# A decoder block on one core: one quarter of a projection moved ahead of the first scores, q and k transfers shared by two queues, and two ScalarE copies placed further back

## The chip, the core and the metric

The kernel runs on one core of a Trainium2 chip. Such a core has five engines that run their own instruction streams in order: TensorE (PE, matrix products, with its weight loads listed as PEld), VectorE (DVE), ScalarE (ACT), GpSimd (POOL) and SyncE (SP). SP and POOL mostly issue DMAs here. The metric is the device time of the whole program in microseconds (us); less is better. The time of a kernel is the median of its runs.

## What is computed

One layer of a decoder block on 256 tokens of width 1024, all in float32. Cut to what matters:

```python
h = rms_norm(x, attn_norm_g)
proj = h @ w_in                      # q,k,v of branch a, q,k,v of branch b, f, g
qa, ka = (partial_rope(rms_norm(split_heads(t, 8), gain)) for t in (qa, ka))
o_a = causal softmax attention(qa, ka, va)       # 8 heads of 64; one block of 256
qb, kb = (rms_norm(split_heads(t, 8), gain) for t in (qb, kb))
c = cumsum(log_sigmoid(f + b_forget))
o_b = causal softmax attention(qb, kb, vb), scores + c[t] - c[s]
gates = sigmoid(g + b_gate)
x = x + (gates[0] * (o_a @ w_branch_moba) + gates[1] * (o_b @ w_branch_fox)) @ w_out
u, g = split(rms_norm(x) @ w_ffn_up);  g = causal_depthwise_conv(g, 3 taps)
x = x + (silu(g) * u) @ w_ffn_down
```

With 256 tokens and blocks of 256 the block selection of branch a selects nothing beyond the token's own block, so branch a is plain causal attention.

## The kernel before

**Weights.** All weights come as chunks of 1 MB (128 x 2048), in the order of the list `chunks`: six projections `qkv` 0 to 5 (q, k, v of branch a, then q, k, v of branch b; two chunks each), eight gate chunks `wg` 0 to 7, then the later matrices. `load` issues a chunk's DMA on SP's queue into one of three buffers `raw`, and cuts it into two quarters of 1024 columns (a quarter of a projection each). Each quarter is split on chip into a high part (`whi`, a copy on ACT, line 134) and a low remainder (`wlo`, a subtraction on DVE, line 135), so that three fast products stand in for one float32 product. `use` asks for a quarter and loads five quarters further ahead (`AHEAD`). The six buffers of `whi` and `wlo` come free as PE finishes quarters.

**Order.** PE's order is that of the code. On DVE, ACT, POOL and SP a scheduler orders the instructions when the program is built, by their place in the code and by its own estimate of when they become ready; `after(i, j)` adds that `i` may not be placed ahead of `j`.

**The stage that the change touches.** `project(m, pt, h)` multiplies two quarters of projection `m` into two PSUM banks; a quarter is 12 matrix products of 128x512. There are 8 banks in all. `finish_qk` normalises a projected q or k: squares on ACT, sums and scalings on DVE, which frees the two banks. `start_turn` transposes 32x32 blocks on DVE and then moves the blocks with 16 DMAs of 32 KB from one half of the tile `pp` to the other; `end_turn` copies the result with a gain on ACT into `qT0`, `kT0`, `qT1` or `kT1` (the digit is the branch). The names `q0`, `k0` are branch a, `q1`, `k1` branch b.

PE's order around the change: k of branch b is projection 4. Three of its four quarters are multiplied, then the small product of `forget_c` (cumulative sum, one bank, which DVE then copies at line 361), then the scores of branch a for three pairs of heads (`scores(0, pair)`, two banks a pair, needing `qT0` and `kT0`), then the fourth quarter, then v of branch b (projection 5), `gate(0)`, the transposes of probabilities `turn(0, 0)` and `turn(0, 1)`, the fourth pair's scores, `gate(1)`, `gate(2)`, `gate(3)`, `turn(0, 2)` and `turn(0, 3)`, and then branch b's scores (`first_half`, `second_half`). A `gate` is two quarters of a gate chunk's projection, and two of them share two banks; DVE moves the result out at line 484 (into `lead`).

For branch a the 16 DMAs of a `start_turn` go alternately to POOL's and SP's queue; for branch b all 16 go to POOL's.

Of the kernel before, what the change touches and what calls it, by code (L numbers as in the profile page):

```python
# [11 lines left out]
AF = mybir.ActivationFunctionType  # L12
ALU = mybir.AluOpType
AX = mybir.AxisListType
# [9 lines left out]
NH = 8  # L24
# [18 lines left out]
def decoder_block(ctx, tc, a, out):  # L43
    nc = tc.nc
# [6 lines left out]
    def T(shape, tag, bufs=1, dt=F32):  # L51
        return sb.tile(shape, dt, tag=tag, bufs=bufs, name=tag)
# [34 lines left out]
    state = {"next": 0, "raw": None, "ahead": AHEAD, "hold": False, "behind": None}  # L87

    def after(i, j):
        tc.add_manual_dep(i.ins, j.ins.name, mybir.DependencyInfo(mybir.DependencyClass.NoSync, mybir.DependencyReason.DATA), reason="order")  # L90
# [25 lines left out]
    def load(upto):  # L116
        while state["next"] <= min(upto, 2 * len(chunks) - 1):
            i, h = divmod(state["next"], 2)
            state["next"] += 1
            if i < 2:  # L120
                lead(2 * i + h)
                continue
            c = chunks[i]
            if h == 0:
                w = 1024 if i == 2 else 2048
                src = a[c[0]]
                for j in (c[1] - (c[0] == "qkv"), *c[2:]):
                    src = src[j]
                raw = state["raw"] = T([P, 2048], "raw", RB)
                for j in range(2048 // w):  # L130
                    nc.sync.dma_start(raw[:, j * w:(j + 1) * w], src[:, j * w:(j + 1) * w])
            raw = state["raw"][:, h * 1024:(h + 1) * 1024]
            hi, lo = home(2 * i + h)
            whi = nc.scalar.activation(hi, raw, AF.Copy)  # L134
            wlo = nc.vector.tensor_tensor(lo, raw, hi.bitcast(F32), op=ALU.subtract)  # L135
            if state["behind"]:
                for i, j in zip((whi, wlo), state["behind"]):
                    if j:
                        after(i, j)
            split[c, h] = (hi, lo, whi)  # L140

    def use(c, h):
        if not state["hold"]:
# [8 lines left out]
    def col(c, n=1):  # L152
        return sm[:, c:c + n]
# [36 lines left out]
    mask3 = cst[:, 384:768]  # L190
# [46 lines left out]
    def project(m, pt, h, quarters=(0, 1)):  # L237
        for hh in quarters:
            wh, wl = use(("qkv", m, h) if isinstance(m, int) else m, hh)
            for k2 in range(2):  # L240
                k = 4 * h + 2 * hh + k2
                rh, rl = (pairs(w[:, k2 * 512:(k2 + 1) * 512]) for w in (wh, wl))
                parts = ((xh, rh), (xl, rh), (xh, rl)) if m == 0 else ((xh, rh), (xh, rl), (xl, rh))
                for i, (lhs, rhs) in enumerate(parts):
                    for t in range(NT):
                        nc.tensor.matmul(pt[t], lhs[:, k, t * P:(t + 1) * P], rhs, start=(k == 0 and i == 0), stop=(k == KT - 1 and i == 2))  # L246
# [4 lines left out]

    last_norm = []

    def finish_qk(pt, br, isk):

        qn = T([P, NT, NH, HD], "qn", 3)
        ss = T([P, NT, NH], "ss", 2)
        for t in range(NT):
            sq = T([P, W4], "sq", 2)
            nc.scalar.activation(sq, pt[t], AF.Square, scale=rs[:, t:t + 1])  # L260
            nc.vector.tensor_reduce(ss[:, t], sq.rearrange("p (h d) -> p h d", h=NH), axis=AX.X, op=ALU.add)
        f = T([P, NT, NH], "qf", 2)
        rsqrt_mean(f.rearrange("p t h -> p (t h)"), ss.rearrange("p t h -> p (t h)"), HD, [NT * NH], "qfv")
        for t in range(NT):
            nc.vector.tensor_scalar(f[:, t], f[:, t], rs[:, t:t + 1], 1.0 if isk else -HD ** -0.5, op0=ALU.mult, op1=ALU.mult)  # L265
            nc.vector.tensor_tensor(qn[:, t], pt[t].rearrange("p (h d) -> p h d", h=NH),
                                    f[:, t, :, None].to_broadcast([P, NH, HD]), op=ALU.mult)
        if br == 0:
            rc, rsn = rope[isk]
            p1 = T([P, NT, NH, 16], "p1", 1)  # L270
            p2 = T([P, NT, NH, 16], "p2", 1)
            x16 = qn[:, :, :, 0:16]
            nc.vector.tensor_tensor(p1, x16, rc[:, :, None, :].to_broadcast([P, NT, NH, 16]), op=ALU.mult)
            nc.vector.tensor_tensor(p2, x16, rsn[:, :, None, :].to_broadcast([P, NT, NH, 16]), op=ALU.mult)
            nc.vector.tensor_tensor(qn[:, :, :, 0:8], p1[:, :, :, 0:8], p2[:, :, :, 8:16], op=ALU.add)
            nc.vector.tensor_tensor(qn[:, :, :, 8:16], p1[:, :, :, 8:16], p2[:, :, :, 0:8], op=ALU.add)
        return qn
# [4 lines left out]

    work = T([P, 4, 1024], "pp")

    def start_turn(n, isk, behind=None, queues=(nc.gpsimd,)):
        y = work[:, 2 * isk].rearrange("p (r t d i) -> p r t d i", r=4, t=NT, d=4)
        raw = work[:, 2 * isk + 1].rearrange("p (t b d i) -> p t b d i", t=NT, b=4, d=4)
        for t in range(NT):
            src = n[:, t].rearrange("p h d -> p (h d)").rearrange("p (d r j) -> p d r j", d=4, r=4)
            i = nc.vector.transpose(y[:, :, t].rearrange("p r d i -> p d r i"), src)  # L290
            if behind:
                after(i, behind)
        for b in range(4):
            for r in range(4):
                queues[r % len(queues)].dma_start(raw[32 * r:32 * (r + 1), :, b], y[32 * b:32 * (b + 1), r])  # L295
        return raw.rearrange("p t b d i -> p d (t b) i")

    def end_turn(raw, br, isk):
        dst = T([P, 4, S], f"{'qk'[isk]}T{br}")
        gain = col(C_QG + 2 * br + isk)  # L300
        nc.scalar.activation(dst.rearrange("p d (c i) -> p d c i", i=32), raw, AF.Copy, scale=gain)
        turned[br, isk] = dst


    bias = T([P, NH, 384], "bias")
# [69 lines left out]
    heads = [pp[:, 0], pp[:, 1]]  # L375
    probs = {}
    last_exp = []

    halved = {}

# [33 lines left out]
    def softmax(br, pair, sps):  # L414
        s = T([P, 2, 384], "s", 4)
        nm = T([P, 2, 2], "nm", 4)
        l = T([P, 2, 2], "l", 4)
        for j in range(2):
            h = 2 * pair + j
            sp = sps[j]  # L420
            for i, c in enumerate((slice(0, 128), slice(128, 384))):
                nc.vector.tensor_tensor_reduce(s[:, j, c], sp[:, c], mask3[:, c] if br == 0 else bias[:, h, c],  # L422
                                               scale=1.0, scalar=3e38, op0=ALU.add, op1=ALU.min, accum_out=nm[:, j, i:i + 1])
            for i, c in enumerate((slice(0, 128), slice(128, 384))):
                last_exp[:] = [nc.scalar.activation(s[:, j, c], s[:, j, c], AF.Exp, scale=-1.0, bias=nm[:, j, i:i + 1], accum_out=l[:, j, i:i + 1])]  # L425
        r = T([P, 2, 2], "r", 4)
        nc.vector.reciprocal(r, l)
        for j in range(2):
            for i, c in enumerate((slice(0, 128), slice(128, 384))):
                last_norm[:] = [nc.vector.tensor_scalar_mul(s[:, j, c], s[:, j, c], r[:, j, i:i + 1])]  # L430
        probs[br, pair] = s
# [41 lines left out]
    def gate(c, late=False):  # L473
        g, h = divmod(c, 2)
        if h == 0:
            state["gate"] = banks()
        project(("wg", c), state["gate"], h, (0,))
        state["hold"] = state["hold"] or late
        project(("wg", c), state["gate"], h, (1,))
        if late:  # L480
            state["hold"] = False
        if h == 1:
            for t in range(NT):
                nc.vector.scalar_tensor_tensor(gates[t][g], state["gate"][t], rs[:, t:t + 1], bg[g], op0=ALU.mult, op1=ALU.add)
# [11 lines left out]
    pq, pk, pv = banks(), banks(), banks()  # L496
# [2 lines left out]
    project(1, pk, 0)  # L499
    norm1()  # L500
    forget_products()
    q0 = start_turn(finish_qk(pq, 0, 0), 0, None, (nc.gpsimd, nc.sync))
    project(1, pk, 1)
    k0 = start_turn(finish_qk(pk, 0, 1), 1, None, (nc.gpsimd, nc.sync))
    project(2, pv, 0)
    project(2, pv, 1)
    finish_v(pv, 0)
    pq = banks()
# [4 lines left out]
    q1 = finish_qk(pq, 1, 0)  # L513
    pk = banks()
# [1 line left out]
    gate_bias()  # L516
    end_turn(q0, 0, 0)
    end_turn(k0, 0, 1)
    project(4, pk, 1, (0,))
    forget_c()  # L520
    for pair in range(3):
        scores(0, pair)
    q1 = start_turn(q1, 0, last_norm[0])
    project(4, pk, 1, (1,))
    k1 = start_turn(finish_qk(pk, 1, 1), 1)
    pv = banks()
    project(5, pv, 0)
    project(5, pv, 1)
# [4 lines left out]
    forget_bias()  # L533
    load(2 * pos["wg", 1] + AHEAD)
    state["behind"] = None
    gate(1)
    end_turn(q1, 1, 0)
    end_turn(k1, 1, 1)
    halve(1)
    gate(2)  # L540
    gate(3, True)
    turn(0, 2)
    state["behind"] = turn(0, 3), None
# [362 lines left out]
```

## Time and profile before

| | us |
|---|---|
| median of three runs | 354.53 |
| lowest and highest | 353.32 and 355.88 |
| the profiled execution | 354.96 |
| its span from first to last instruction | 353.2 |
| outside the span | 1.8 |

| engine | busy us | share of the span |
|---|---|---|
| PE | 343.9 | 97% |
| DVE | 296.5 | 84% |
| ACT | 220.2 | 62% |
| POOL | 26.8 | 8% |

The mean TensorE clock granted in this execution is 0.994 of full speed. Rows of a timeline give start, duration, engine, line, operation, what it writes and reads, how many instructions are merged, and in brackets the idle time of the engine before the row with what ended it. Rows of a table of stretches give the stretch, its length, the busy time of PE, PEld, DVE, ACT and POOL with instruction counts, the granted TensorE clock, the share of the DMA engines and GB/s.

### The profile page before, as it was taken

To read this page: it belongs to the slowest core of one execution; us is meant where nothing else is said; L and a number is where in the kernel's file an instruction comes from. 1 tells how busy PE (TensorE), PEld (TensorE's weight loads), DVE (VectorE), ACT (ScalarE), POOL (GpSimd) and SP (SyncE) were. 2 spreads that over 40 slices of the span, in tenths; PEclk is the share of its full clock that TensorE was granted. 3 is DMA by queue.
4 is the path that set the end of the run, shared out by engine and by line. 5 is a ranking of instruction groups with operands and counts; after the bars stand their busy time and mean duration, and the time that the engine had idled before them with its cause. 6 is when DMAs were issued, how large, how long until landed. Compare 5 with 4: busy or idle time off the path is not lost.

```text
span 353.2 us, 5443 instructions
## 1 busy us (share of the span) xinstructions
PE 343.9 (97%) x1983; PEld 300.2 (85%) x1983; DVE 296.5 (84%) x562; ACT 220.2 (62%) x384; POOL 26.8 (8%) x56
## 2 busy tenths in 40 slices
PE   8999997998989999999999999999999999999995
PEld 4878886886878888888999989999898989989885
DVE  5899999892999848896989999788897897968963
ACT  4867656862959837645785865676566664755630
POOL 0000260078300000000000000000000000000000
PEclk9999999999899999999999999999999999999999
DMA  7988868667461625668427457367464566457003
GB/s 286 392 328 259 290 187 293 228 211 242 147 253 47 239 119 201 205 228 305 149 104 292 186 181 272 144 229 238 139 228 155 205 237 216 158 179 258 26 0 119
DMA packets 17226, 72.19 MB, mean 204 GB/s; under 512 B 2856, under 2 KB 7088, under 8 KB 9776
## 3 DMA queue, kind: packets, MB, share of 16 engines
q1 hardware_dynamic: 14464, 69.22, 55.1%
q0 software_dynamic: 1536, 1.58, 1.8%
q10 hardware_dynamic: 1200, 1.06, 0.9%
q8 instruction: 15, 0.25, 0.3%
q14 instruction: 11, 0.09, 0.1%
HBM read 67.64 MB, written 1.06 MB: 195 GB/s over the span
## 4 chain that ended last, share of the span: by engine, by line
PE 70%; DMA 11%; DVE 8%; ACT 5%; issue 2%; SPq 2%; POOL 1%; ACTq 0%; POOLq 0%
PE bank L642 26%; PE bank L781 16%; PE bank L643 13%; DMA raw<-in_qkv 6%; PE bank L593 6%; PE bank L246 6%; DMA pp<-pp 4%; DVE wlo L135 3%; PE bank L458 2%; SPq L295 2%; ACT s L425 1%; ACT whi L134 1%; DMA lead<-in_lead 1%; POOL pp L295 1%; DVE bias L371 1%
## 5 line engine op out<-in xcount | busy, mean ns | idle before, releaser
L135 DVE TENSOR_TENSOR wlo<-raw,whi 128x1024 fp32r<-128x1024 f32 x94 | 113.6, 1218 | 7.2 <-ACT whi L134 6.9
L134 ACT ACTIVATE whi<-raw 128x1024 fp32r<-128x1024 f32 x94 | 97.2, 1050 | 19.7 <-DMA raw<-in_wu 5.2
L246 PE MATMUL bank<-whi,x 128*128 128x512 f32 x320 | 85.2, 386 | 2.2 <-ACT pT L434 1.8
L642 PE MATMUL bank<-pp,whi 128*128 128x512 f32 x232 | 76.6, 382 | 0.0
L246 PEld LDWEIGHTS bank<-whi,x 128*128 128x128 f32 x320 | 60.8, 192 | 13.2 <-ACT pT L434 2.3
L643 PE MATMUL bank<-pp,wlo 128*128 128x256 f32 x232 | 63.2, 273 | 0.0
L642 PEld LDWEIGHTS bank<-pp,whi 128*128 128x128 f32 x232 | 43.8, 189 | 6.1
L246 PE MATMUL bank<-wlo,x 128*128 128x512 f32 x160 | 48.6, 386 | 0.1
L643 PEld LDWEIGHTS bank<-pp,wlo 128*128 128x128 f32 x232 | 44.5, 192 | 0.2
L246 PEld LDWEIGHTS bank<-wlo,x 128*128 128x128 f32 x160 | 30.2, 191 | 5.4 <-DVE wlo L103 0.8
L295 POOL DMA_DIRECT2D pp<-pp x48 | 25.5, 538 | 45.9 <-DVE qf L265 22.6
L781 PE MATMUL bank<-whi,qT 128*128 128x512 f32 (+1 forms) x92 | 27.8, 370 | 0.0
L755 ACT ACTIVATE s<-sq,sm 128x256 f32<-128x256 f32 x22 | 13.1, 597 | 17.3 <-DVE sq L751 17.3
L750 DVE TENSOR_TENSOR sq<-bank,lows 128x256 f32<-128x256 f32 x44 | 18.0, 415 | 6.3 <-ACT lows L749 6.2
L758 ACT ACTIVATE s<-s 128x256 f32<-128x256 f32 x22 | 9.1, 415 | 17.3 <-DVE s L757 17.3
L781 PEld LDWEIGHTS bank<-whi,qT 128*128 128x128 f32 x92 | 17.2, 189 | 2.3
L642 PE MATMUL bank<-pp,bias 128*128 128x512 f32 x56 | 18.7, 382 | 0.0
L781 PE MATMUL bank<-wlo,qT 128*128 128x512 f32 (+1 forms) x46 | 17.0, 370 | 0.0
L593 PE MATMUL bank<-whi,pp 128*128 128x512 f32 x64 | 17.0, 382 | 0.0
L749 ACT ACTIVATE lows<-bank 128x256 f32<-128x256 f32 x44 | 15.6, 366 | 1.1 <-PE bank L643 1.1
L751 DVE TENSOR_TENSOR sq<-sq,rsB 128x512 f32<-128x512 f32 x22 | 15.2, 689 | 0.5
L425 ACT ACTIVATE s<-s,nm 128x128 f32<-128x128 f32 (+1 forms) x32 | 14.1, 451 | 1.9 <-DVE nm L422 1.9
(180 smaller groups left out, 576.0 us busy)
## 6 DMA issues: line engine op xcount, KB each, us to landing
raw<-in_wu SPq DMA_DIRECT2D x22, 1024.0 KB, 4.8
raw<-in_wd SPq DMA_DIRECT2D x11, 1024.0 KB, 5.0
raw<-in_qkv SPq DMA_DIRECT2D x9, 1024.0 KB, 6.4
raw<-in_wg SPq DMA_DIRECT2D x8, 1024.0 KB, 5.7
raw<-in_wb SPq DMA_DIRECT2D x4, 1024.0 KB, 4.8
raw<-in_wo SPq DMA_DIRECT2D x4, 1024.0 KB, 4.7
lead<-in_lead SPq DMA_DIRECT2D x8, 384.0 KB, 6.1
pp<-pp POOLq DMA_DIRECT2D x48, 32.0 KB, 3.3
```

The lines of the kernel that those rows point to most:

```text
L134: whi = nc.scalar.activation(hi, raw, AF.Copy)
L135: wlo = nc.vector.tensor_tensor(lo, raw, hi.bitcast(F32), op=ALU.subtract)
L246: nc.tensor.matmul(pt[t], lhs[:, k, t * P:(t + 1) * P], rhs, start=(k == 0 and i == 0), stop=(k == KT - 1 and i == 2))
L295: queues[r % len(queues)].dma_start(raw[32 * r:32 * (r + 1), :, b], y[32 * b:32 * (b + 1), r])
L425: last_exp[:] = [nc.scalar.activation(s[:, j, c], s[:, j, c], AF.Exp, scale=-1.0, bias=nm[:, j, i:i + 1], accum_out=l[:, j, i:i + 1])]
L593: nc.tensor.matmul(ps_[t], lhs[:, t * P:(t + 1) * P], rhs, start=(k == 0 and i == 0), stop=(k == 3 and i == 2))
L642: nc.tensor.matmul(two[i], wh[:, c], both, start=(k == 0), stop=False)
L643: nc.tensor.matmul(two[i][:, 0:S], wl[:, c], high, start=False, stop=(k == KT - 1))
L749: nc.scalar.activation(lows[:, i:i + 1].rearrange("p b (a t) -> p b a t", a=2), apart(two[i][:, S:2 * S], 1), AF.Copy)
L750: nc.vector.tensor_tensor(halves(ev[:, i:i + 1]), apart(two[i][:, 0:S], 1), halves(lows[:, i:i + 1]), op=ALU.add)
L751: nc.vector.tensor_tensor(ev, ev, rs2[:, None, :].to_broadcast([P, 2, S]), op=ALU.mult)
L781: nc.tensor.matmul(o, lhs, rhs, start=(first and i == 0), stop=(end and i == 2))
```

## The change

It does four things.

1. Projection 4's fourth quarter is multiplied together with its third, ahead of `forget_c` and the three pairs of scores.
2. All q and k transfers are issued alternately on POOL and SP: 16 transfers of branch b (8 of q1, 8 of k1) move from POOL's queue to SP's.
3. The sums of squares of k1 (DVE) may not be placed ahead of the row maximum of the third pair's scores.
4. ACT's copy into `qT1` may not be placed ahead of the fourth pair's exponentials; ACT's copy into `kT1` and the split `halve(1)` move behind `gate(2)` in the code, the copy not ahead of the last `whi` loaded there.

```diff
-    def finish_qk(pt, br, isk):
+    def finish_qk(pt, br, isk, behind=None):
...
-            nc.vector.tensor_reduce(ss[:, t], sq.rearrange("p (h d) -> p h d", h=NH), axis=AX.X, op=ALU.add)
+            i = nc.vector.tensor_reduce(ss[:, t], sq.rearrange("p (h d) -> p h d", h=NH), axis=AX.X, op=ALU.add)
+            if behind:
+                after(i, behind)
...
-    def start_turn(n, isk, behind=None, queues=(nc.gpsimd,)):
+    def start_turn(n, isk, behind=None, queues=(nc.gpsimd, nc.sync)):
...
-    def end_turn(raw, br, isk):
+    def end_turn(raw, br, isk, behind=None):
...
-        nc.scalar.activation(dst.rearrange("p d (c i) -> p d c i", i=32), raw, AF.Copy, scale=gain)
+        i = nc.scalar.activation(dst.rearrange("p d (c i) -> p d c i", i=32), raw, AF.Copy, scale=gain)
+        if behind:
+            after(i, behind)
...
-    project(4, pk, 1, (0,))
+    project(4, pk, 1)
     forget_c()
     for pair in range(3):
         scores(0, pair)
     q1 = start_turn(q1, 0, last_norm[0])
-    project(4, pk, 1, (1,))
-    k1 = start_turn(finish_qk(pk, 1, 1), 1)
+    k1 = start_turn(finish_qk(pk, 1, 1, last_max[0]), 1)
...
+    end_turn(q1, 1, 0, last_exp[0])
     gate(1)
-    end_turn(q1, 1, 0)
-    end_turn(k1, 1, 1)
+    gate(2)
+    end_turn(k1, 1, 1, state["whi"])
     halve(1)
-    gate(2)
     gate(3, True)
```

What the scheduler makes of it is shown at three places. Lines shift by up to six in the changed program (361 becomes 366, 422 becomes 428, 301 becomes 304, 434 becomes 440, 295 becomes 298).

**DVE, just ahead of the first scores of branch a, before.** The tile `pT_677` with 8 partitions is the cumulative sum that `forget_c` leaves in a bank; `raw_632` is the last chunk of projection 5 and `raw_770` the first gate chunk; the ISA rows are the row maxima of the first pair.

```order
L135 TENSOR_TENSOR wlo_659<-raw_632,whi_658 128x1024
L361 COPY pT_677<-bank_674 8x256
L362 TENSOR_SCALAR pT_677<-pT_677 8x128
L422 ISA s_689,nm_690<-bank_683,cst_172 128x128
...
L422 ISA s_689,nm_690<-bank_684,cst_172 128x256
...
L135 TENSOR_TENSOR wlo_773<-raw_770,whi_772 128x1024
```

The same place with the change; here the first gate chunk is `raw_674`.

```order
L135 TENSOR_TENSOR wlo_659<-raw_632,whi_658 128x1024
L135 TENSOR_TENSOR wlo_677<-raw_674,whi_676 128x1024
L366 COPY pT_695<-bank_692 8x256
L367 TENSOR_SCALAR pT_695<-pT_695 8x128
L428 ISA s_707,nm_708<-bank_701,cst_172 128x128
...
L428 ISA s_707,nm_708<-bank_702,cst_172 128x256
```

The low part of the first gate quarter stood behind the first pair's four maxima and now stands ahead of the copy and of these maxima.

**ACT, from the last split ahead of the transposed probabilities on, before.** `raw_916` is the fourth gate chunk, `raw_1009` the fifth and `raw_1058` the sixth; `pT_934` is the first of the two copies of `turn(0, 0)`; the rows of line 425 are the fourth pair's exponentials.

```order
L134 ACTIVATE whi_918<-raw_916 128x1024
L301 ACTIVATE qT1_1029<-pp_178,sm_79 128x1024
L386 ACTIVATE qn_1033<-qT1_1029 128x512
L434 ACTIVATE pT_934<-bank_935 128x6x64
...
L425 ACTIVATE s_974,l_976<-s_974,nm_975 128x256
L134 ACTIVATE whi_1011<-raw_1009 128x1024
L134 ACTIVATE whi_1042<-raw_1009 128x1024
L301 ACTIVATE kT1_1031<-pp_178,sm_79 128x1024
L386 ACTIVATE qn_1034<-kT1_1031 128x1024
L134 ACTIVATE whi_1060<-raw_1058 128x1024
```

The same place with the change; `raw_1011` is the fifth gate chunk and `raw_1049` the sixth.

```order
L134 ACTIVATE whi_918<-raw_916 128x1024
L440 ACTIVATE pT_934<-bank_935 128x6x64
...
L431 ACTIVATE s_974,l_976<-s_974,nm_975 128x256
L304 ACTIVATE qT1_997<-pp_178,sm_79 128x1024
L134 ACTIVATE whi_1013<-raw_1011 128x1024
L392 ACTIVATE qn_1069<-qT1_997 128x512
L134 ACTIVATE whi_1033<-raw_1011 128x1024
L134 ACTIVATE whi_1051<-raw_1049 128x1024
L304 ACTIVATE kT1_1067<-pp_178,sm_79 128x1024
L392 ACTIVATE qn_1070<-kT1_1067 128x1024
```

The copy into `qT1` has moved from ahead of the transposed probabilities to behind the fourth pair's exponentials, and the copy into `kT1` from behind the fifth chunk's split to behind the first split of the sixth.

**SP, from the last q and k transfers of branch a on, before.** Rows of 32x2x128 are q and k transfers, rows of 128x2048 weight chunks.

```order
L295 DMA pp_178<-pp_178 32x2x128 x8
L131 DMA raw_770<-in_wg 128x2048
L131 DMA raw_844<-in_wg 128x2048
L131 DMA raw_878<-in_wg 128x2048
L131 DMA raw_916<-in_wg 128x2048
L131 DMA raw_1009<-in_wg 128x2048
L131 DMA raw_1058<-in_wg 128x2048
```

The same place with the change.

```order
L131 DMA raw_674<-in_wg 128x2048
L131 DMA raw_844<-in_wg 128x2048
L131 DMA raw_878<-in_wg 128x2048
L131 DMA raw_916<-in_wg 128x2048
L298 DMA pp_178<-pp_178 32x2x128 x8
L131 DMA raw_1011<-in_wg 128x2048
L298 DMA pp_178<-pp_178 32x2x128 x8
L131 DMA raw_1049<-in_wg 128x2048
```

Eight transfers of q1 now stand ahead of the fifth gate chunk on SP's queue, and eight of k1 ahead of the sixth.

More of the change, by code (lines that the diff above doesn't have):

```diff
@@ L140, in load @@
             split[c, h] = (hi, lo, whi)
+            state["whi"] = whi
     def use(c, h):
@@ L377, in decoder_block @@
     last_exp = []
+    last_max = []
     halved = {}
@@ L421, in softmax @@
             for i, c in enumerate((slice(0, 128), slice(128, 384))):
-                nc.vector.tensor_tensor_reduce(s[:, j, c], sp[:, c], mask3[:, c] if br == 0 else bias[:, h, c],
-                                               scale=1.0, scalar=3e38, op0=ALU.add, op1=ALU.min, accum_out=nm[:, j, i:i + 1])
+                last_max[:] = [nc.vector.tensor_tensor_reduce(s[:, j, c], sp[:, c], mask3[:, c] if br == 0 else bias[:, h, c],
+                                               scale=1.0, scalar=3e38, op0=ALU.add, op1=ALU.min, accum_out=nm[:, j, i:i + 1])]
             for i, c in enumerate((slice(0, 128), slice(128, 384))):
@@ L501, in decoder_block @@
     forget_products()
-    q0 = start_turn(finish_qk(pq, 0, 0), 0, None, (nc.gpsimd, nc.sync))
+    q0 = start_turn(finish_qk(pq, 0, 0), 0)
     project(1, pk, 1)
-    k0 = start_turn(finish_qk(pk, 0, 1), 1, None, (nc.gpsimd, nc.sync))
+    k0 = start_turn(finish_qk(pk, 0, 1), 1)
     project(2, pv, 0)
```

## The prediction

> **What bounds the kernel now.** I read the page's busy times first, then PE's timeline for its waits, then the granted clock by stretches, then the timelines of ACT, DVE and the two DMA queues around each wait.
>
> ```profile
> PE 343.9 (97%) x1983; PEld 300.2 (85%) x1983; DVE 296.5 (84%) x562; ACT 220.2 (62%) x384; POOL 26.8 (8%) x56
> 56.13 0.59 PE L246 MATMUL bank<-whi,x 128*128 128x512 f32 x2
> 56.86 0.60 PE L359 MATMUL bank<-cst,lf 128*8 128x128 f32 x4
> 59.11 0.49 PE L394 MATMUL bank<-kT,qT 64*128 64x128 f32 x4 [1.64 <-ACT kT L301]
> 60.52 0.39 PE L394 MATMUL bank<-kT,qT 64*128 64x128 f32 x4
> 61.27 0.70 PE L246 MATMUL bank<-whi,x 128*128 128x512 f32 x2
> 62.24 1.03 PE L246 MATMUL bank<-whi,x 128*128 128x512 f32 x4
> 63.54 1.03 PE L246 MATMUL bank<-whi,x 128*128 128x512 f32 x4
> 86.06 0.59 PE L246 MATMUL bank<-whi,x 128*128 128x512 f32 x2
> 88.41 0.86 PE L246 MATMUL bank<-whi,x 128*128 128x512 f32 x2 [1.75 <-ACT pT L434]
> 100.81 0.97 PE L444 MATMUL bank<-cst,s 64*128 64x64 f32 x24
> 101.62 0.44 PE L394 MATMUL bank<-kT,qT 64*128 64x128 f32 x4
> 102.98 0.49 PE L394 MATMUL bank<-kT,qT 64*128 64x128 f32 x4 [0.92 <-DVE lead L484]
> ```
>
> PE is busy for 97% of the span. In the whole timeline only these three rows after the start show a wait: 1.64 us for `kT0` ahead of the first scores, 1.75 us ahead of `gate(2)`, 0.92 us ahead of branch b's second pair. From 102.98 us to the end PE never waits, so what the change is worth is what it does to these three.
>
> ```profile
> 56.00:60.00 4.00, 2.22 (x20) 1.42 (x20) 3.96 (x11) 1.48 (x3) 0.00 (x0) 1.00 0.89 352
> 88.00:92.00 4.00, 3.59 (x10) 2.81 (x11) 3.96 (x14) 3.81 (x12) 3.07 (x6) 0.67 0.28 62
> 92.00:96.00 4.00, 4.00 (x19) 3.42 (x18) 4.00 (x7) 3.97 (x5) 0.00 (x0) 0.90 0.73 260
> ```
>
> The third number from the end is the granted clock. The second wait is followed by a slow stretch, the first is not (1.00). The clock lost is 4.00 x (0.33 + 0.10) = 1.72 us. PE's pace says the same: six products take 63.54 - 62.24 = 1.30 us, so the 48 of `gate(2)` and `gate(3)` should take 10.38 us and took 100.81 - 88.41 = 12.40, which is 2.02 more, some 0.3 of it the refill after a wait. The second wait thus costs 1.75 + 2.02 = 3.77 us.
>
> **First part: the quarter ahead of the scores.** PE's total work stays the same. The wait for `kT0` is covered by 12 products of 2.60 us (two rows of six). But the order shows that DVE now makes the first gate quarter's `wlo` ahead of the copy of `forget_c`'s bank.
>
> ```profile
> 59.98 1.06 ACT L134 ACTIVATE whi<-raw 128x1024 fp32r<-128x1024 f32 x1 [0.93 <-DMA raw<-in_wg]
> 58.19 1.22 DVE L135 TENSOR_TENSOR wlo<-raw,whi 128x1024 fp32r<-128x1024 f32 x1
> 59.32 0.41 DVE L361 COPY pT<-bank 8x256 f32<-8x256 f32 x1
> 60.28 0.42 DVE L422 CUSTOM_DVE_ANT_0 s<-bank,cst 128x256 f32<-128x256 f32 x1
> 60.84 0.42 DVE L422 CUSTOM_DVE_ANT_0 s<-bank,cst 128x256 f32<-128x256 f32 x1
> ```
>
> That `wlo` needs the quarter's `whi`, which waits for the chunk's DMA and ends at 59.98 + 1.06 = 61.04; nothing ahead of it moves. The `wlo` starts at 61.10, and as DVE starts its next instruction 59.32 - 58.19 = 1.13 us after such a `wlo`, the copy starts at 62.23 and ends at 62.64. DVE's block from the copy on is 2.91 us later than before.
>
> Who needs the copy? Eight banks: two hold k's unfinished sums, two were q's (freed before 59.32), one holds `forget_c`'s result, three are free. The six score banks of three pairs take the three, the two and the one, so the third pair's second bank is the one that the copy frees. PE gets there early: its quarter ends at 56.13 + 0.43 + 2.60 = 59.16, `forget_c` takes at most 0.60, two pairs 60.52 - 59.11 = 1.41: it asks at 61.2 and waits some 1.4 us. The rest of the third pair takes up to 61.27 - 60.52 = 0.75 us, to 63.4. Then projection 5 needs the first pair's two banks, which its maxima free at 60.28 + 0.42 + 2.91 = 63.61 and 60.84 + 0.42 + 2.91 = 64.17. So its second product starts at 64.2. Before, the fourth quarter's last product was the second in the row at 63.54, and the same second product started at 63.54 + 3 x 0.217 = 64.19. **The gain of the first part is nil**: the wait for `kT0` becomes a wait for the copy and for two maxima. Bounds: a loss of 0.4 if each hand-over costs 0.1 more, a gain of 2.1 (back to the 61.9 at which the shown durations would let PE start projection 5) if no bank were waited for.
>
> What it does to the clock is open. In the 3.0 us from 61.2 to 64.2 PE would be idle for 3.0 - 0.75 - 0.2 = 2.0 us, more than in either of the two waits of the trace, of which one cost the clock and one did not. I take the price of the row: 1.72 us; bounds 0 and 2.02.
>
> **Second part: ACT's copies further back.**
>
> ```profile
> 78.68 1.06 ACT L134 ACTIVATE whi<-raw 128x1024 fp32r<-128x1024 f32 x1 [2.16 <-DMA raw<-in_wg]
> 79.60 0.97 PE L444 MATMUL bank<-cst,s 64*128 64x64 f32 x24
> 86.17 1.15 ACT L301 ACTIVATE qT<-pp,sm 128x1024 f32<-128x1024 f32 x1 [6.42 <-DMA pp<-pp]
> 87.88 0.85 ACT L434 ACTIVATE pT<-bank 128x384 f32<-128x384 f32 x2
> 88.01 0.69 DVE L387 TENSOR_TENSOR qn<-qT,qn 128x512 fp32r<-128x512 f32 x1 [6.23 <-ACT qn L386]
> 102.19 1.40 DVE L484 SCALAR_TENSOR_TENSOR lead<-bank,rs,lows 128x512 f32<-128x512 f32 x2
> ```
>
> ACT stood for 6.42 us at the `qT1` copy, with the copies of `turn(0, 0)` behind it, which free the banks of `gate(2)`; DVE stood for 6.23 us in the same way. With `qT1` behind the fourth pair's exponentials the copies run as soon as PE has transposed (79.60 + 0.97, at the same time as before), at 80.6, take 0.85 and are ready at 81.4, and PE asks at 86.06 + 0.43 = 86.49: five us of cover. The wait and its clock go: **-1.75 and -2.02**.
>
> The third wait came from DVE's backlog: it works without a pause from 88.01 to 103.59 (102.19 + 1.40), 15.58 us, and the first `lead` of `gate(3)` ends 0.65 before. Now it starts earlier:
>
> ```profile
> 62.82 0.18 DVE L427 RECIPROCAL r<-l 128x4 f32<-128x4 f32 x1 [0.21 <-ACT s L425]
> 66.39 0.18 DVE L427 RECIPROCAL r<-l 128x4 f32<-128x4 f32 x1 [0.48 <-ACT s L425]
> 68.14 0.18 DVE L427 RECIPROCAL r<-l 128x4 f32<-128x4 f32 x1 [0.53 <-ACT s L425]
> 69.28 1.30 DVE L290 STREAM_TRANSPOSE pp<-qn 128x512 f32<-128x512 f32 x2
> 78.24 1.30 DVE L290 STREAM_TRANSPOSE pp<-qn 128x512 f32<-128x512 f32 x2
> 79.46 2.32 DVE L135 TENSOR_TENSOR wlo<-raw,whi 128x1024 fp32r<-128x1024 f32 x2
> ```
>
> The 58.19 to 79.54 stretch holds the same instructions in both orders, with 0.21 + 0.48 + 0.53 = 1.2 us of pauses before; now it resumes at 61.10 with the first `wlo` done, so k1's transposes end, if no pause is left, at 61.10 + 21.35 - 1.2 - 1.13 = 80.1. Two `wlo` (2.3) and the same 15.58 us follow: first `lead` at 97.3. PE arrives at 86.49 + 10.38 + (101.62 - 100.81) + 0.25 = 97.9. So **-0.92**, with 0.6 us to spare, bound 0.
>
> **Third part: the queues.**
>
> ```profile
> 71.15 6.46 POOL L295 DMA_DIRECT2D pp<-pp  x12 [17.47 <-ACT whi L134]
> 79.18 2.12 POOL L295 DMA_DIRECT2D pp<-pp  x4 [1.57 <-DMA pp<-pp]
> 42.08 6.02 SPq L295 DMA_DIRECT2D pp<-pp  x8
> 88.61 1.02 DVE L446 COPY pT<-bank 128x384 f32<-128x384 f32 x2
> 91.15 0.49 ACT L425 ACTIVATE s<-s,nm 128x256 f32<-128x256 f32 x1
> 108.02 0.70 PE L246 MATMUL bank<-whi,x 128*128 128x512 f32 x2
> pp<-pp POOLq DMA_DIRECT2D x48, 32.0 KB, 3.3
> DMA to landing us min/median/max: 4.7/5.0/7.6
> ```
>
> POOL took from 71.15 to 81.30 for q1's 16 issues; SP takes 6.0 us for eight. q1's transposes ended at 70.58 and end near 73.5 now, later by the 2.9 of the maxima that they follow. So q1 is issued by 79.5 and landed 3.3 later by 82.8. `qT1`'s copy comes only behind the fourth pair's exponentials, which ended 91.64 - 88.61 = 3.0 us after DVE began `turn(0, 1)`'s copies; these now begin at 80.1 + 2.3 = 82.4, so `qT1` starts at 85.4 and nothing waits. k1: transposed at 80.1, issued by 86.3, landed by 89.6. Behind k1's eight on SP stands the sixth gate chunk, and ACT's order has its `whi` ahead of `kT1`'s copy. Issued at 86.3 and landing after the median 5.0 us of weight chunks (the last row, in the stretch 30 to 125): 91.3, `whi` 1.06, `kT1` 1.15, split 1.07, on DVE 1.13 twice and the first `lead` 0.74: 97.6, still ahead of PE's 97.9. Fifth and sixth chunk are first multiplied in `gate(4)`, at 108.02 before, some 5 us earlier now, so their own delay costs nothing. **0.**
>
> **Sum.** 0 (first wait moved) + 1.72 (its clock) - 1.75 - 2.02 - 0.92 = -2.97. The profiled execution took 354.96 (0.43 above the median of 354.53), so **352.0 us**.
>
> **Rivals.**
>
> A, the forecast: the new wait costs the clock, 352.0. For: more idle time than in the wait that did.
>
> B, it keeps the clock: 354.96 - 4.69 = 350.3. For: the first wait, 1.64 us, kept 1.00. Against: the 1.75 us one did not.
>
> [...]
>
> C, the first part works as its words say and the copy is in time: 64.2 back to 61.9 + 0.2, no clock lost: 350.3 - 2.1 = 348.2. Against: the order on DVE, and 59.98.
>
> D, slower: the sixth gate chunk lands late. At the 7.6 us of the slowest chunk the chain above ends at 100.2, so PE waits 2.3 us for the bank and may lose the clock again: 352.0 + 2.3 + 1.72 = 356.0. It decides from a landing of 5.3 us on, and is slower than before from about 6.6 on. For: 32 transfers share the DMA engines near it. Against: its neighbours on the queue are issued before it, and the median is 5.0.
>
> **Chances.** A 0.52, B 0.24, C 0.08, D 0.16. A range that holds eight times in ten runs from C, 348.4, to a D without a second loss of clock, 354.9. One per cent, about what a measurement of this kernel can tell from no change, is 3.5 us, so faster by over 1% means below 351.0: most of B and C and a fifth of A, 0.38. Slower by over 1% (above 358.1) takes more than D: 0.04. Within: 0.58.
>
> **What will show it.** Right if PE's row of the third pair's scores waits for DVE's copy (line 366) and not for `kT0`; if projection 5 starts at 64 us; if `gate(2)` follows `gate(1)` without a wait and the clock between 86 and 97 us is 1.00; if a dip of the clock, or none, follows 61 to 65 us. Wrong if the copy comes before the first gate quarter's `wlo`, if `kT1` is late, or if PE waits anywhere after 104 us, where it never did.

## The result and the profile after

| | before | with the change |
|---|---|---|
| median of six runs, us | 355.20 | 349.83 |
| lowest and highest | 353.32 and 359.34 | 349.10 and 350.72 |
| the profiled execution | 354.96 | 350.03 |
| its span, and its mean clock | 353.2, 0.994 | 348.3, 1.000 |

The ratio is 0.9856, with a 95% interval of 0.9818 to 0.9894: the change makes the kernel 1.4% faster, by 4.9 us between the two profiled executions. The ratios here and below leave out runs more than 1.5% above the fastest of their kernel, while medians and extremes are of all runs. The six runs of the kernel before are the three of its first table and three more. The forecast of 352.0 was 2.0 us above the profiled execution and 2.2 us above the median; rival B's 350.3 is what came.

The page's line of busy times, which differs from that of before mainly in POOL's (26.8 us and 56 instructions there):

```profile
PE 342.0 (98%) x1983; PEld 299.8 (86%) x1983; DVE 297.1 (85%) x562; ACT 222.3 (64%) x384; POOL 18.3 (5%) x40
```

PE's timeline around the three places where it waited before (start, duration, line, tile, and in brackets the wait ahead of the row):

```profile
59.51 0.49 PE L400 MATMUL bank<-kT,qT 64*128 64x128 f32 x4
...
62.24 0.37 PE L400 MATMUL bank<-kT,qT 64*128 64x128 f32 x1 [0.93 <-DVE pT L366]
...
63.10 1.04 PE L247 MATMUL bank<-whi,x 128*128 128x512 f32 x2
63.97 0.59 PE L247 MATMUL bank<-wlo,x 128*128 128x512 f32 x2
...
85.64 1.03 PE L247 MATMUL bank<-whi,x 128*128 128x512 f32 x4
...
97.33 0.73 PE L400 MATMUL bank<-kT,qT 64*128 64x128 f32 x7
...
102.73 0.70 PE L247 MATMUL bank<-whi,x 128*128 128x512 f32 x2
```

One wait is left, and it is the predicted one: the third pair's scores wait for DVE's copy (line 366), no longer for `kT0`. `gate(2)` at 85.64 and branch b's scores at 97.33 follow without a wait, and `gate(4)` starts at 102.73 instead of 108.02. The table of stretches shows the clock behind the new wait and behind `gate(2)`:

```profile
60.00:64.00 4.00, 3.00 (x24) 2.04 (x22) 3.33 (x12) 3.60 (x9) 0.00 (x0) 1.00 0.97 398
...
88.00:92.00 4.00, 4.00 (x20) 3.50 (x19) 4.00 (x5) 2.13 (x3) 0.00 (x0) 1.00 0.94 394
92.00:96.00 4.00, 4.00 (x20) 3.50 (x19) 3.53 (x4) 1.98 (x2) 0.00 (x0) 1.00 0.88 294
```

It is 1.00 everywhere, where 0.67 and 0.90 stood before.

### The profile page after: what moved, and what is told of

The parts are those of the page before. It is cut to its first block, busy times and chain, and to the rows that moved or that the text cites. A ratio compares the mean times of both kernels' runs of the same rounds, so it can differ in the third digit from the quotient of the medians.

```text
span 348.3 us, 5440 instructions
## 1 busy us (share of the span) xinstructions
PE 342.0 (98%) x1983; PEld 299.8 (86%) x1983; DVE 297.1 (85%) x562; ACT 222.3 (64%) x384; POOL 18.3 (5%) x40
## 4 chain that ended last, share of the span: by engine, by line
PE 81%; DMA 9%; DVE 4%; ACT 2%; SPq 2%; issue 1%; ACTq 0%
PE bank L647 26%; PE bank L786 16%; PE bank L247 15%; PE bank L648 13%; PE bank L598 6%; DMA raw<-in_qkv 6%; DVE wlo L135 2%; SPq L298 2%; PE bank L464 2%; DMA lead<-in_lead 1%; DMA raw<-in_wg 1%; ACT whi L134 1%; PE bank L450 1%; ACT qn L180 1%; PE bank L413 0%
## 5 line engine op out<-in xcount | busy, mean ns | idle before, releaser
L247 PE MATMUL bank<-whi,x 128*128 128x512 f32 x320 | 84.1, 382 | 0.6 <-ACT whi L102 0.5
L247 PEld LDWEIGHTS bank<-whi,x 128*128 128x128 f32 x320 | 60.0, 189 | 11.1 <-ACT whi L102 1.2
L247 PE MATMUL bank<-wlo,x 128*128 128x512 f32 x160 | 47.9, 381 | 0.0
L298 POOL DMA_DIRECT2D pp<-pp x32 | 17.0, 540 | 47.4 <-DVE qf L268 22.9
```

## The experiments

Twelve kernels were run, each with runs of the kernel before beside it on the same chip; the ratio is to those. The kernel before had medians of 353.96 us beside 1 to 4, 354.43 beside 5 to 8, 354.86 beside 9 to 11 and 354.89 beside 12, so medians of different groups compare to about 1 us.

| | median (lowest to highest), us | ratio (95% interval) |
|---|---|---|
| the change | 349.83 (349.10 to 350.72) | 0.9856 (0.9818 to 0.9894) |
| 1: order of the copies alone | 355.11 (349.98 to 358.39) | 0.9993 (0.9942 to 1.0045) |
| 2: quarter and queues | 349.16 (348.71 to 350.06) | 0.9845 (0.9803 to 0.9888) |
| 3: order and queues | 349.43 (349.16 to 350.00) | 0.9852 (0.9811 to 0.9893) |
| 4: the change, first gate split later | 347.94 (347.83 to 348.10) | 0.9807 (0.9766 to 0.9847) |
| 5: queues alone | 349.54 (348.62 to 352.33) | 0.9874 (0.9838 to 0.9909) |
| 6: quarter and order | 358.44 (357.12 to 358.88) | 1.0103 (1.0074 to 1.0131) |
| 7: as 4, copies in the old order | 348.79 (348.51 to 348.99) | 0.9837 (0.9809 to 0.9865) |
| 8: the kernel before again | 354.42 (352.99 to 357.48) | 1.0009 (0.9983 to 1.0035) |
| 9: k1's transfers shared alone | 354.67 (353.70 to 356.88) | 1.0000 (0.9972 to 1.0028) |
| 10: q1's transfers shared alone | 353.59 (350.46 to 356.32) | 0.9948 (0.9909 to 0.9986) |
| 11: POOL and ScalarE | 356.77 (354.73 to 357.97) | 1.0053 (1.0022 to 1.0084) |
| 12: SP alone | 357.83 (356.10 to 358.51) | 1.0073 (1.0023 to 1.0122) |

### 1: the order of the copies alone

The change without the quarter and without the shared queues (the first and third part of the prediction). The rule on k1's sums of squares stays in, here and in 2, 3, 4, 6 and 7:

```diff
-    project(4, pk, 1)
+    project(4, pk, 1, (0,))
     forget_c()
...
-    q1 = start_turn(q1, 0, last_norm[0])
-    k1 = start_turn(finish_qk(pk, 1, 1, last_max[0]), 1)
+    q1 = start_turn(q1, 0, last_norm[0], (nc.gpsimd,))
+    project(4, pk, 1, (1,))
+    k1 = start_turn(finish_qk(pk, 1, 1, last_max[0]), 1, None, (nc.gpsimd,))
```

> Only the order of ScalarE's copies of branch b's q and k is changed; the quarter stays behind the scores and branch b's transfers on POOL's queue. Theory 1 (the order of the copies brings the gain: 1.75 us of wait ahead of gate(2), some 1.7 to 2.0 us of clock behind it, 0.92 us of the third wait): 354.96 - 4.7 = 350.3, PE's wait of 1.64 us for kT0 still there, no wait at 88 us. Theory 2 (the copies were late because q1's transfers were late, and the order alone only hands the wait on to qT1 or kT1 further back): the third wait of 0.92 us stays or grows, because k1's 16 transfers alone on POOL's queue land some 4 us later than when shared: 351 to 354.

Measured: 355.11, no gain. This kernel's timeline, first a row of PE, then ACT's two copies, then DVE:

```profile
100.84 0.70 PE L400 MATMUL bank<-kT,qT 64*128 64x128 f32 x4 [3.66 <-DVE lead L490]
...
85.54 1.15 ACT L304 ACTIVATE qT<-pp,sm 128x1024 f32<-128x1024 f32 x1 [1.72 <-DMA pp<-pp]
...
95.49 1.15 ACT L304 ACTIVATE kT<-pp,sm 128x1024 f32<-128x1024 f32 x1 [5.44 <-DMA pp<-pp]
...
97.77 1.23 DVE L393 TENSOR_TENSOR qn<-kT,qn 128x1024 fp32r<-128x1024 f32 x1 [4.67 <-ACT qn L392]
```

The wait ahead of `gate(2)` is gone, as predicted, and its price is not saved. PE is early at the next place and waits there: k1's transfers arrive at 95.49, ScalarE stands 5.44 us for them, DVE behind it 4.67 us, and `gate(3)`'s `lead`, queued behind on DVE, frees the bank only for 100.84. Theory 2 holds: the wait was handed on. The time is 1 us above its 351 to 354.

### 2 and 3: the change without the order, and without the quarter

Experiment 2 puts the copies back to their old place; experiment 3 puts the quarter back behind the scores.

```diff
-    end_turn(q1, 1, 0, last_exp[0])
     gate(1)
-    gate(2)
-    end_turn(k1, 1, 1, state["whi"])
+    end_turn(q1, 1, 0)
+    end_turn(k1, 1, 1)
     halve(1)
+    gate(2)
```

> The changed kernel with ScalarE's copies of branch b's q and k in the old order; quarter and shared queues as changed. Theory 1 (the order of the copies brings the gain): the copy into qT1 holds up the copies of turn(0, 0) again, PE waits ahead of gate(2), and the clock may go: 350.0 + 1.75 + 1.9 + 0.9, up to 354.6, at least 351.8 with the clock kept. Theory 2 (the shared queues alone remove it): q1 is landed at 79.2 us with shared queues, its copy ends at 80.3 and turn(0, 0)'s copies at 82, PE asks at 85.6: no wait, 350.0 within 0.5.

> The changed kernel with projection 4's fourth quarter back behind the scores. If the first part is worth its measured 0.4 us (projection 5's second product at 63.7 instead of 64.2): 350.4, with PE's wait for kT0 of some 1.6 us at 59 us and none for the third pair's bank. If the wait for kT0 sometimes costs the clock: single runs near 352. If the first part also was needed to clear DVE's backlog ahead of gate(3): the 0.92 us wait is back, 351.3.

Measured: 349.16 and 349.43, both as fast as the whole change. In experiment 2 ScalarE's old order does no harm, since q1 arrives at 78.14, in ACT's timeline:

```profile
78.14 1.15 ACT L304 ACTIVATE qT<-pp,sm 128x1024 f32<-128x1024 f32 x1 [1.62 <-DMA pp<-pp]
...
79.86 0.85 ACT L440 ACTIVATE pT<-bank 128x384 f32<-128x384 f32 x2
```

The copies of `turn(0, 0)` run at 79.86, some 5 us before `gate(2)` starts on PE. Theory 1 falls; theory 2's step holds, at a time 0.8 below its 350.0 where 0.5 was allowed. In experiment 3 PE waits 0.69 us for `kT0` and 0.4 us for `lead`, no run lies near 352: the quarter is worth nothing that these runs can tell.

### 4 and 7: what holds PE after the quarter

The load of the first gate quarter is asked for behind the first pair's scores, and its low part may not be placed ahead of their maxima. Experiment 7 is the same with the copies of experiment 2.

```diff
-    project(4, pk, 1)
+    project(4, pk, 1, (0,))
+    state["hold"] = True
+    project(4, pk, 1, (1,))
+    state["hold"] = False
     forget_c()
-    for pair in range(3):
-        scores(0, pair)
+    scores(0, 0)
+    state["behind"] = None, last_max[0]
+    load(2 * pos["qkv", 4, 1] + 1 + AHEAD)
+    state["behind"] = None
+    scores(0, 1)
+    scores(0, 2)
```

> The changed kernel with the low part of the first gate quarter behind the first pair's four maxima on DVE, as it stood before the change, so that the copy of forget_c's bank no longer waits for the gate chunk's DMA. If the wlo is what holds PE (my step on the first part): the copy ends before 60 us, PE asks for the bank at 61.2 and does not wait, projection 5 starts at 62 instead of 63.1: 350.0 - 1.4 = 348.6 (348.2 to 349.3). If PE is held by something else there, kT0 or the maxima: 350.0 within 0.3.

> The fourth experiment (low part of the first gate quarter behind the first pair's maxima) with ScalarE's copies of branch b's q and k in the old order. If the order of the copies is worth nothing once the transfers are early: 347.9 within 0.3. If it gives cover against late landings: single runs up to 349.5, where the fourth experiment's lay between 347.83 and 348.10.

Measured: 347.94 and 348.79. The first two fences are the change's ACT and DVE at the copy, the third is experiment 4's DVE and PE:

```profile
59.55 1.06 ACT L134 ACTIVATE whi<-raw 128x1024 fp32r<-128x1024 f32 x1 [0.56 <-DMA raw<-in_wg]
```

```profile
60.64 1.23 DVE L135 TENSOR_TENSOR wlo<-raw,whi 128x1024 fp32r<-128x1024 f32 x1 [1.46 <-ACT whi L134]
61.78 0.40 DVE L366 COPY pT<-bank 8x256 f32<-8x256 f32 x1
```

```profile
59.30 0.41 DVE L366 COPY pT<-bank 8x256 f32<-8x256 f32 x1 [1.62 <-PE bank L364]
...
61.36 0.70 PE L247 MATMUL bank<-whi,x 128*128 128x512 f32 x2
```

With the change the copy stands behind a `wlo` that waits for a chunk; without that it ends 2.5 us earlier (0.3 of it because that execution is as much ahead on PE) and PE runs through. Projection 5's first product comes at 61.36 instead of 63.10. The runs of the change reach over 1.62 us and those of experiment 4 over 0.27, perhaps because the chunk's arrival no longer counts. This version is faster than both kernels, and 0.3 below the 348.2 to 349.3 expected. In experiment 7 PE waits 0.19 us for `lead` at 96.37 and the runs lie between 348.51 and 348.99; neither of the two patterns expected came. The order may give some tenths once nothing else is late, but 4 and 7 did not run side by side, and their ratios' intervals overlap.

### 5 and 6: the queues alone, and the rest without them

Experiment 5 is the kernel before with only the default queues of `start_turn` changed; experiment 6 is the change with POOL's queue alone for branch b.

```diff
-    def start_turn(n, isk, behind=None, queues=(nc.gpsimd,)):
+    def start_turn(n, isk, behind=None, queues=(nc.gpsimd, nc.sync)):
```

> The kernel before with nothing changed but the queues: branch b's q and k transfers alternate between POOL's and SP's queue. Theory 3 (the late transfers are the cause, the third part alone brings the gain): q1 landed by about 79, k1 by about 87 us, no wait ahead of gate(2) and none of 3 us ahead of branch b's second pair; the wait for kT0 (0.7 to 1.6 us at 58 us) stays: 349.0 to 350.5. Theory 4 (the queues bring it only together with one of the other parts): a wait ahead of gate(2) is left, 351.5 to 354.

> The changed kernel with branch b's transfers back on POOL's queue alone; quarter and order of the copies as changed. Theory 3: k1's last transfer lands at about 95 us as in the first experiment, DVE's subtraction for kT1 holds up lead, PE waits about 3 us near 97 us and often loses clock: 352.5 to 356. Theory 4 (quarter and order together do without the shared queues): 350 within 0.5.

Measured: 349.54 and 358.44. **The queues alone bring the gain, and without them the other two parts make the kernel 1% slower.** PE's waits in experiment 5, and PE and ACT in experiment 6:

```profile
58.19 0.49 PE L394 MATMUL bank<-kT,qT 64*128 64x128 f32 x4 [1.50 <-ACT kT L301]
...
98.62 0.49 PE L394 MATMUL bank<-kT,qT 64*128 64x128 f32 x4 [1.35 <-DVE lead L484]
```

```profile
100.11 0.80 PE L400 MATMUL bank<-kT,qT 64*128 64x128 f32 x4 [4.21 <-ACT kT L304]
...
104.25 0.80 PE L400 MATMUL bank<-kT,qT 64*128 64x128 f32 x4 [3.34 <-DVE lead L490]
...
98.91 1.15 ACT L304 ACTIVATE kT<-pp,sm 128x1024 f32<-128x1024 f32 x1 [9.35 <-DMA pp<-pp]
```

The profiled execution of experiment 5 keeps two short waits and no slow clock; one of its six runs, 352.33, had a mean clock of 0.994. Experiment 5 also lacks the rule on k1's sums of squares, so the gain does not need that either. In experiment 6 k1 arrives at 98.91, and PE stands twice, 7.55 us in all. Theory 3 holds; experiment 6 is worse than it said.

### 8: the kernel before again

No edit.

> The kernel before itself, for the clock granted in each run and a second profile. [...] Theory L (the length of the wait decides, from about 1.7 us on): every execution loses the clock after its longest wait, the runs all near 0.994.

Measured: twelve runs with mean clocks from 0.988 to 1.000, three of them at 1.000; span times clock spreads over 3 us, so it is not the clock alone that differs. The second profile shows another pattern than the first, at the same time (354.88 against 354.96), in PE's and ACT's timeline:

```profile
101.31 0.49 PE L394 MATMUL bank<-kT,qT 64*128 64x128 f32 x4 [3.94 <-DVE lead L484]
...
83.17 1.15 ACT L301 ACTIVATE qT<-pp,sm 128x1024 f32<-128x1024 f32 x1 [4.34 <-DMA pp<-pp]
...
94.82 1.16 ACT L301 ACTIVATE kT<-pp,sm 128x1024 f32<-128x1024 f32 x1 [4.19 <-DMA pp<-pp]
```

Here q1 comes 3 us earlier than in the profile that I read, there is no wait ahead of `gate(2)` at all, and k1's late arrival costs 3.94 us at the second pair. The 1.75 and 0.92 us of the first profile and this 3.94 are one cause, late transfers, seen at two places. Theory L, by which every run loses the clock, falls as it was stated with the three runs at 1.000; these have no profile, so whether they had a long wait is not known.

### 9 to 12: why two queues are faster

In 9 and 10 the kernel before shares only k1's, or only q1's transfers; in 11 and 12 all of branch b's go to other queues.

```diff
 9: k1 = start_turn(finish_qk(pk, 1, 1), 1, None, (nc.gpsimd, nc.sync))
10: q1 = start_turn(q1, 0, last_norm[0], (nc.gpsimd, nc.sync))
11: (nc.gpsimd, nc.scalar) for q1 and k1
12: (nc.sync,) for q1 and k1
```

> The kernel before with k1's 16 transfers alternating between POOL's and SP's queue, q1's still on POOL's alone. If k1's late landing (94 to 95 us) is what costs the most: k1 landed by about 88.5 us (POOL's eight stand behind q1's until 81), the wait at 97 us falls to 1.4 us or less, a wait of 0 to 1.8 us ahead of gate(2) for q1 may stay: 349.5 to 352. If q1's landing decides: 352 to 354.

> The kernel before with q1's 16 transfers shared, k1's on POOL's queue alone. q1 landed by about 78 us, no wait ahead of gate(2). k1 begins at 79.4 without q1's backlog, 16 issues of 0.53 end at 88 us, landing 91 to 94: if k1's landing decides, PE waits 1.5 to 3.5 us at 97 us: 351 to 354. If q1's backlog was the whole delay of k1: 349.5 to 350.5.

> The kernel before with branch b's transfers alternating between POOL's and ScalarE's queue, so that SP sends the weight chunks as early as before. If the shared queues gain by halving the time of the issues: q1's last transfer lands about 1.5 us after its last issue, at 77 to 79 us, and k1's by 88. If they gain by holding back the 1 MB weight chunks behind which small transfers queue: q1's transfers land in clumps 3 to 6 us after their issue, the last near 82 to 83 us when the second chunk in flight lands, and k1's after 90. The total is not clean, since ScalarE issues 16 transfers and its order moves: 349 to 355.

> The kernel before with all 32 transfers of branch b on SP's queue, so that one engine issues them all, as in the kernel before, but no weight chunk can be issued between the 16 of a turn. If a weight chunk in flight is what keeps small transfers waiting: q1's transfers land 1.3 to 2.2 us after their issue without a gap, the last near 82 us, though issued over 10 us; k1's, issued behind one more chunk, lag 4 us while it flies and 1.5 after, the last near 92 us. If a single queue as such is slow: lags of 3 to 6 us for q1 as on POOL's. The total: k1 still late by the serial issue, a wait of 1 to 4 us for lead or kT1 and often a loss of clock, 351 to 356.

Measured: 354.67, 353.59, 356.77, 357.83. One transfer set alone helps little. PE and ACT in 9, then in 10:

```profile
100.68 0.80 PE L394 MATMUL bank<-kT,qT 64*128 64x128 f32 x4 [2.57 <-DVE lead L484]
...
83.85 1.15 ACT L301 ACTIVATE qT<-pp,sm 128x1024 f32<-128x1024 f32 x1 [4.72 <-DMA pp<-pp]
```

```profile
98.92 0.49 PE L394 MATMUL bank<-kT,qT 64*128 64x128 f32 x4 [1.71 <-DVE lead L484]
...
92.44 1.15 ACT L301 ACTIVATE kT<-pp,sm 128x1024 f32<-128x1024 f32 x1 [5.02 <-DMA pp<-pp]
```

In 9, `kT1`'s copy starts at 90.61, yet q1 is as late as before (83.85), DVE stands for it, and a wait of 2.57 us is left; I had said 349.5 to 352, or 352 to 354 if q1 decides; the time is above both. In 10, k1 is late (92.44), as said.

For the reason of the lateness, the DMA view of each kernel over the stretch of q1's issues: tile, queue, count, size, and median us from issue to landing. First before, then the change, 11 and 12:

```profile
raw<-in_wg SPq DMA_DIRECT2D x3, 1024.0 KB, 5.7
pp<-pp POOLq DMA_DIRECT2D x16, 32.0 KB, 4.8
```

```profile
raw<-in_wg SPq DMA_DIRECT2D x1, 1024.0 KB, 5.2
pp<-pp SPq DMA_DIRECT2D x8, 32.0 KB, 1.9
pp<-pp POOLq DMA_DIRECT2D x8, 32.0 KB, 1.8
```

```profile
raw<-in_wg SPq DMA_DIRECT2D x1, 1024.0 KB, 8.3
pp<-pp ACTq DMA_DIRECT2D x8, 32.0 KB, 7.1
pp<-pp POOLq DMA_DIRECT2D x8, 32.0 KB, 6.6
```

```profile
pp<-pp SPq DMA_DIRECT2D x16, 32.0 KB, 1.9
```

Where weight chunks are in flight beside them, the 32 KB transfers of q1 need a median of 4.8 us before (4.3 in the second profile) and 6.6 to 7.1 in 11, nearly as long as the chunks' 5.7 (5.5) and 8.3; where none is, 1.9 in 12 and in the change (whose one chunk there is issued behind the last of them) and 2.3 in experiment 5. POOL's queue as such is not slow: it has 1.8 in the change. One queue alone (12) is no hindrance to the landing either: SP's 16 transfers keep the next chunk back, in the program's order, and land in 1.9 us. The timeline of SP's queue over the same stretch, in experiment 5, in 12, and before (the duration is that of the issues):

```profile
69.92 6.18 SPq L295 DMA_DIRECT2D pp<-pp  x8
76.20 1.01 SPq L131 DMA_DIRECT2D raw<-in_wg  x2
```

```profile
69.97 11.68 SPq L295 DMA_DIRECT2D pp<-pp  x16
```

```profile
72.90 19.33 SPq L131 DMA_DIRECT2D raw<-in_wg  x4
```

Shared queues do two things at once: 16 transfers are issued in 6 us instead of 10 to 12, and the next chunk waits until they are. Neither alone brings q1 sooner, as the time from its first issue to the start of `qT1`'s copy shows, which waits for it in each of these profiles. It is 15.0 and 12.5 us in the two profiles of the kernel before, 12.3 in 11 with the issues halved (80.38 less 68.08), 13.2 in 12 with no chunk in flight (83.21 less 69.97), and 7.7 and 7.3 in 5 and 10, which have both.

The totals of 11 and 12 say less, as each has a cost of its own, and both lie above what was expected (349 to 355 and 351 to 356). ACT in 11, then PE in 12:

```profile
80.38 1.15 ACT L301 ACTIVATE qT<-pp,sm 128x1024 f32<-128x1024 f32 x1 [0.53 <-DMA pp<-pp]
...
81.57 5.41 ACTq L295 DMA_DIRECT2D pp<-pp  x8
```

```profile
103.82 0.96 PE L394 MATMUL bank<-kT,qT 64*128 64x128 f32 x3 [6.40 <-ACT pT L434]
```

In 11 ScalarE issues k1's transfers for 5.41 us; the copies of `turn(0, 0)` stand behind them until 87.03, and PE waits 4.06 us at 102.01. In 12 the chunks are issued behind k1's transfers, from 93.02 on, ACT waits for them with `turn`'s copies behind, and PE stands 6.40 us. By these profiles, one of each kernel and two of before, q1's earlier landing needs both, the halved issues and the chunk held back. How the gain of the whole kernel divides between them is not shown.

k1 gains in another way. In the first profile of before its transfers take a median of 1.8 us, but POOL issues them only from 82.07 to 91.07, behind q1's. In the change they take 4.2 (SP) and 3.8 us (POOL) beside the fifth gate chunk, but are issued from 79.14 to 84.59. So k1 gains by the earlier issue and not by a faster landing.

## Why the prediction was right or wrong

**The first wait, right.** The copy waits for the first gate quarter's `wlo` and PE for the copy. Projection 5's second product starts at about 63.75 (63.97 less a product's pace of 0.22) instead of the predicted 64.2, since the chunk came earlier: `whi` starts at 59.55, not 59.98. That is a gain of some 0.4, within my bounds, and by experiment 3 it can't be told from nothing.

**Its clock, +1.72: the term that spoiled the sum.** I took the price of the 1.75 us wait for a wait of about 2.0 us of idle time. PE's idle time was 0.93 and some 0.4 between projection 5's first and second product, and no run of the change had a mean clock below 0.999. Without this term the sum is 354.96 - 4.69 = 350.3, and with the 0.4 of the first part 349.9, against 350.03 measured. The forecast gave faster by over 1%, which is what came, a chance of 0.38.

**The second part, -1.75 -2.02 -0.92: right in the sum, wrong in the cause.** The step "with `qT1` behind the fourth pair's exponentials the copies run as soon as PE has transposed" is what experiment 1's trace shows. What I did not price is the same step with the queues left as they were: k1 then arrives at 95.5, and everything that was saved is lost at the second pair. In the changed kernel the copies' order is not what removes the wait ahead of `gate(2)`, since experiment 2 has the old order and no wait. The 4.69 us belong to the third part. That they come out so well is partly luck: they are the waits of one execution, and the second profile of the same kernel, at the same total, had 3.94 us at the second pair in place of the 1.75 and 0.92.

**The third part, 0: wrong.** I asked whether the shared queue hurts anything and not what late transfers cost in the kernel before, though the rows with 6.42 us <-DMA on ACT stood there. I also took 3.3 us from issue to landing, a median over 48 transfers of three situations; with no chunk in flight it was 1.9, so that q1's last transfer landed at 79.2 instead of by 82.8. For k1 3.3 was near: its transfers took 3.8 to 4.2.

**Two slips of arithmetic.** Forty-eight products at 1.30 us for six are 10.40 us, not 10.38, which changes nothing. The range's ends, 348.4 and 354.9, are not quite the times of the rivals that they are named after: C is 348.2, and D without a second loss of clock 352.0 + 2.3 = 354.3.

**Rival D** did not come: the sixth gate chunk took 5.0 us, and the fifth 5.2. **Rival C's** price, 348.2, was right for the kernel in which the copy is in time: experiment 4 took 347.94. **No wait** appeared past 104 us.

## What to carry to other kernels

A wait in a profile names the instruction that was last, in that execution; before pricing its removal, follow the released engine to the next consumer of the same late data, and take a second profile to see whether the wait stands still. When an in-order engine waits on a DMA, first ask why the DMA is late: here q1's small transfers were in flight beside 1 MB loads and k1's stood behind q1's, and issuing half of them on the loads' own queue, ahead of the next load, was worth 1.3% alone, where reordering the engine that waited brought nothing measurable (experiments 5 and 1). Code moved for cover can also bring forward a prefetch whose arrival then stands ahead of something urgent, as the `wlo` ahead of the copy did.

## What the runs showed of the hardware

**The clock.** In the first profile of before the clock falls to half speed for 3.41 us (89.37 to 92.78, 0.50), in experiment 6 for three such pieces in a row; a piece in which PE is busy throughout costs 1.7 us of work, half of 3.41. The table of stretches in pieces of that length, counted from the slow ones (second column after the length: PE's busy time; third from the end: the clock), for the first profile of before, for the second, and for experiment 6:

```profile
85.95:89.37 3.42, 1.67 (x8) 0.99 (x7) 1.36 (x3) 3.17 (x5) 3.08 (x7) 1.00 0.27 60
89.37:92.78 3.41, 3.41 (x10) 2.70 (x9) 3.38 (x15) 3.22 (x11) 1.70 (x4) 0.50 0.22 48
```

```profile
95.35:98.76 3.41, 2.02 (x32) 1.44 (x31) 2.20 (x3) 3.38 (x4) 0.00 (x0) 1.00 0.58 204
98.76:102.17 3.41, 0.86 (x14) 0.86 (x16) 3.16 (x4) 3.41 (x7) 0.00 (x0) 1.00 0.59 219
102.17:105.58 3.41, 3.41 (x30) 2.92 (x30) 3.38 (x18) 3.25 (x16) 0.00 (x0) 0.50 0.87 342
```

```profile
96.44:99.85 3.41, 0.00 (x0) 0.00 (x0) 0.00 (x0) 0.94 (x1) 0.00 (x0) 0.99 0.03 11
99.85:103.26 3.41, 0.80 (x4) 0.51 (x4) 2.08 (x2) 3.38 (x7) 0.00 (x0) 0.50 0.00 0
103.26:106.67 3.41, 2.42 (x22) 2.42 (x24) 2.54 (x10) 2.85 (x6) 0.00 (x0) 0.50 0.61 185
106.67:110.08 3.41, 3.41 (x28) 2.69 (x27) 3.41 (x18) 3.39 (x16) 0.00 (x0) 0.51 0.51 202
```

At full clock, a piece in which PE was busy for 1.67 us was followed by a slow one, a piece with 2.02 was not; nor was one with 2.06 in the first profile of before (55.27 to 58.68). In experiment 1 a piece with 0.14 us (97.57 to 100.98) stood ahead of the slow one. That the work in such a piece decides, and at what border, is not shown by so few.

The wait of 3.94 us, spread over two pieces, cost one slow piece, as the 1.75 us wait did, which lay in one. The wait of 1.64 us in the first profile of before left 2.06 us of work in one piece and 2.98 in the next (58.68 to 62.09) and cost none. Experiment 10's wait of 1.71 us cost none by PE's pace: the 32 products of line 458 (464 in the change) take 2.82 us at 101.21, as in the change at 99.98, where the clock was 1.00. The length of the wait parts these as well, so that it matters where a wait falls is not shown. The slow pieces do not lie alike in each execution: those of the two profiles of before start 12.80 us apart, which is no multiple of 3.41. Experiment 6's third row, busy for 2.42 us at half clock and followed by another slow piece, stays unexplained.

**The DMA engines.** I had not expected 32 KB transfers on another queue to take as long as the 1 MB chunk beside them (7.1 and 8.3 us in experiment 11). With half of the issues on ScalarE, that experiment saved only time of the issues: they took 6 us instead of 10 to 12, and the transfers took 6.6 to 7.1 us to land. Sharing with SP gained more for q1, 7.3 us from its first issue to its copy in experiment 10 against 12.3 in 11, and there the order on SP's queue also held the next chunk back.
